# A hybrid decoder layer on one core: another order of the mixer's products

## The chip, the cores and the metric

The kernel runs on one core of one Trainium2 chip. The metric is the device time of one execution in microseconds; three executions of the kernel before gave 1690.62, 1692.16 and 1694.79 us (median 1692.16).

## What is computed

One inference step of one decoder layer in float32, for a prompt of 512 tokens and 8 samples of 4 tokens: 544 columns of width 1024. Cut to what matters here:

```
x += 0.5 * SwiGLU_1(rms(x))                  # feed-forward, width 2816
u  = rms(x) @ w_in                           # one combined projection
A: sliding-window attention, 12 heads of 128 in 3 groups (dilation 1, 4, 16),
   the three heads of a slot merged by their softmax denominators
B: gated delta rule, 8 heads of 128, causal convolution of width 4 on q/k/v,
   chunked exact form, head norm, gate silu(z)
x += (sig(gA) * (oA @ w_proj_a) + sig(gB) * (oB @ w_proj_b)) @ w_out
x += 0.5 * SwiGLU_2(rms(x));   y = rms(x)
```

The outputs are y, the new keys and values, the convolution rows and the delta-rule states, for prompt and samples.

## The kernel before

Activations stand transposed, features on the 128 partitions and the 544 columns in two halves h of 272. A *unit* is one 128-row block of one product for one half: 8 (or 4, or 11) weight tiles of 128x128, three matmuls per tile. Weights and activations are split in a rounded part and a rest (`split_next`, line 428; tiles G, xh, xl, hh), and a unit sums hi*hi, hi*lo and lo*hi, so one tile costs three matmuls of 272 columns. `unit` (line 613) issues them. The weights of four tiles form a group G: ACT rounds it, VectorE or GpSimd subtracts to get the rest.

`make_plan` (line 155) writes down the units: first feed-forward, then `ba` (the two logits of the delta rule), then the mixer, then the output projections `pa`, `pb`, `wo`, then the second feed-forward. The mixer's order is the table `MIX_ORDER` (line 43): ("a", i) stands for attention head i = 3*slot + group, that is the six units q, k, v times two halves; ("p", i) for delta-rule head i, six units; ("z", n) for the gate block n of the delta rule, two units; ("t", n) for the four units of output gate n. Unit names below are those of the plan: `gdn 4 2 0` is delta-rule head 4, its third product (v), half 0; `at 3 2 1 0` is slot 3, group 2, key, half 0; `z 0 1` and `gate 3 1 1` end with the half.

The work behind the products (*side work*) is written as generators: `conv`, `gating`, `gdn_pair` (two delta-rule heads at a time), `gdn_sample`, `attn_slot`, `attn_sample`. A generator yields between its steps. After every weight tile `unit` calls `pump` (line 647), which lets those generators go one step that a planner (class `Meter`) holds to be ready; their matmuls then stand in TensorE's queue between two matmuls of the unit. Storage of 544 columns (tag S, `CFG["S"]` tiles) is counted in `live`; a generator that needs tiles yields in `need` (line 288) until there is room. Where a unit itself cannot go on (its convolution buffers are full, or `z_load` cannot reserve its tiles) `until` (line 294) calls `force` (line 667), which lets the side work run, step behind step, until the condition holds. TensorE's queue is in order.

The norms: `norm_acc` (538) squares on ACT and adds on GpSimd, `norm_fin` (584) sums over the partitions by a matmul with ones and takes the inverse square root on VectorE (`rsqrt`, 392). At the start eight weight groups are split ahead, then the first norm runs while the first units already multiply. `store_y` (605) is the last norm's multiplication. All engine calls go through one line of `Meter` (line 122), so every row of the profile shows L122; tiles tell the rows apart.

Names in the rows: mm, sd are PSUM tiles; X, Y, Pm, Q, B are tiles of the triangular solve in `gdn_pair`, vk its values, r the inverse norm (or a remainder in `gdn_pair`); cache, ex, pT belong to `attn_sample`; st, mk, zm, kf to `gdn_sample`; astf to the merge in `attn_slot`; bas and g to `gating`; mats holds the identity (transposes) and other constants.

Of the kernel before, what the change touches and what calls it, by code (L numbers as in the profile page):

```python
# [17 lines left out]
P = 128  # L18
DM = 1024
KT = 8  # L20
# [18 lines left out]

CFG = dict(S=62, S2=4, G=4, G2=8, RAW=2, U3=3, H=10, HM=6, LA=4, LAG=3.0, SLACK=0.0, BANKS=3, PRE=3, LOV=("pa", "pb", "ba", "z", "gate", "gdn", "at"), CV=0, WARM=4, EP=8, DUE=2, RES=0, RQ="gpsimd")  # L40


MIX_ORDER = [("a", 0), ("p", 0), ("p", 1), ("p", 2), ("a", 1), ("p", 3), ("a", 2), ("a", 3), ("p", 4), ("a", 4), ("p", 5), ("a", 5)]
MIX_ORDER += [("p", 6), ("a", 6), ("p", 7), ("a", 7), ("a", 8), ("a", 9), ("a", 10), ("a", 11)]
MIX_ORDER += [("z", n) for n in range(6)] + [("t", n) for n in range(4)] + [("z", n) for n in (6, 7)]

# [159 lines left out]
def consts():  # L206
# [35 lines left out]
    m4 = ((i % 4)[:, None] == np.arange(4)[None, :]).astype(np.float32)  # L242
    mats = np.concatenate([ident, tri, negm, tri_s, neg_s, ones_s, m1, one, hb, mb, mh, cs, by4, by4.T, m4], 1)
    at = np.concatenate(t0 + [t1, t2, ts], 1)
# [18 lines left out]
class Builder:  # L263
# [214 lines left out]
    def build(self):  # L478
        nc, A = self.nc, self.A
        self.x = [self.S(name="x") for _ in range(KT)]  # L480
        vec = self.C([P, A["in_vec_dram"].shape[1]], name="vec")
        mats = self.C([P, A["in_mats_dram"].shape[1]], name="mats")
        warm = self.H()
        nc.gpsimd.memset(warm, 0.0)
# [15 lines left out]
        for _ in range(CFG["WARM"]):  # L500
            self.mm(ps[:, :NH], warm[:, 0:P], warm)
        names = ["ident", "tri", "negm", "tri_s", "neg_s", "ones_s", "m1", "ones"]
        for k, n in enumerate(names):
# [9 lines left out]
        self.gn = vec[:, 196:197]  # L513
        self.acc, self.r = [None, None], [None, None]
        self.xn = [(self.S(dt=F32R, name="xh"), self.S(dt=F32R, name="xl")) for _ in range(KT)]
# [6 lines left out]
        xw = lambda n, h: self.xw_tile(n, h, 0)  # L522
        seq(xw, 0, {3: (0,), 5: (1,), 7: (0, 1)})
        load_x(1, range(4, KT))
# [13 lines left out]
    def norm_acc(self, n, h):  # L538
        s = self.sl(h)
        if n == 0:  # L540
            self.acc[h] = [self.S([P, NH], name="acc")]
            self.act(self.acc[h][0], self.x[n][:, s], AF.Square)
        else:
            q = self.H()
            self.act(q, self.x[n][:, s], AF.Square)
            if self.last and n == KT - 1 and h == 1:
                self.acc[h].append(q)
            else:
                self.tt(self.acc[h][0], self.acc[h][0], q, ALU.add, self.nc.gpsimd)
        if self.last:  # L550
            self.act(self.x[n][:, s], self.x[n][:, s], AF.Copy, scale=self.wn[3][:, n:n + 1])
# [53 lines left out]
    def store_y(self, h):  # L605
        s = self.sl(h)
        for n in range(KT):
            f = self.H()
            self.tt(f, self.x[n][:, s], self.R(h), ALU.mult, self.nc.gpsimd if n % 3 == 2 else None)
            (self.nc.scalar if n % 2 and h else self.nc.sync).dma_start(self.A["out_y"][:, n, s], f)  # L610
# [70 lines left out]
    def kernel_units(self):  # L681
# [5 lines left out]
        self.xn2, self.normed = [], [False, False]  # L687
        self.use, self.norm_no = [False, False], 0
        for ui, u in enumerate(self.units):
# [8 lines left out]
            pend.append(getattr(self, "u_" + u[0])(*u[1:]))  # L698
            if ui in (3, 6):
                self.norm_fin(ui // 3 - 1)  # L700
            if ui not in (3, 6) and ui < 6:
                continue
# [102 lines left out]
    def u_ba(self, h, wids):  # L805
        ps = self.unit(wids, self.xn, h)

        def evac():
            self.tt(self.bas[:40, self.sl(h)], ps[:40], self.R(h)[:40], ALU.mult)
            if h == 1:  # L810
                self.spawn(self.gating(), self.bas)
        return evac

# [1049 lines left out]
```

## Time and profile before

| | before |
|---|---|
| median of 3 executions | 1692.16 us (1690.62 to 1694.79) |
| the profiled execution | 1692.98 us |
| its span, first to last instruction | 1691.2 us |
| mean granted TensorE clock | 0.985 |
| TensorE busy | 1646.0 us (97%) |
| VectorE, ACT, GpSimd busy | 1010.5, 622.4, 164.5 us |
| moved by DMA | 204.66 MB |

How to read it: PE rows are matmuls, PEld rows the weight loads that overlap them, DVE is VectorE, POOL is GpSimd. PEclk is the granted clock as a share of full speed. A time in square brackets behind a row is how long the engine stood idle just before it, and what ended that.

### The profile page before, as it was taken

The numbers are of one execution on the slowest core, as the hardware profiler recorded it, in microseconds if no ns is written. First come the engines' busy times: TensorE is split into PE (matmuls) and PEld (weight loads), VectorE is DVE, ScalarE is ACT, GpSimd is POOL, SyncE is SP. The second block draws the span as 40 slices with busy tenths as digits, with TensorE's granted clock in tenths as the row PEclk, the third lists the DMA queues.
The fourth block names the chain that finished last, engine by engine and source line by source line (L and its number), as shares of the span: only waits on it lengthen the run. The fifth ranks groups of instructions, "written<-read, shape, count | busy, mean of one in ns | idle before, by whom it ended". The sixth has DMA issues, their size and how long they took to land.

```text
span 1691.2 us, 33645 instructions
## 1 busy us (share of the span) xinstructions
PE 1646.0 (97%) x13389; PEld 1603.8 (95%) x13389; DVE 1010.5 (60%) x2497; ACT 622.4 (37%) x1559; POOL 164.5 (10%) x289
## 2 busy tenths in 40 slices
PE   7999999999999989999999999999999999999996
PEld 7999999999899978988989888999999999999996
DVE  7755255545777977578867467263357554355534
ACT  5332223333454434453534345332243332133332
POOL 5000000001012121022121110000010000000012
PEclk9999999999999979999999999999999999999998
DMA  5222222221524543367455856232332322222221
GB/s 184 84 92 88 91 85 93 83 88 63 174 88 126 191 142 123 125 192 219 132 167 180 292 185 190 88 103 88 119 120 76 100 88 88 88 90 86 93 77 59
DMA packets 105649, 204.66 MB, mean 121 GB/s; under 512 B 20434, under 2 KB 46580, under 8 KB 105492
## 3 DMA queue, kind: packets, MB, share of 16 engines
q1 hardware_dynamic: 93924, 161.97, 29.6%
q0 software_dynamic: 10992, 39.99, 7.7%
q8 instruction: 105, 1.72, 0.4%
q10 hardware_dynamic: 576, 0.56, 0.1%
q14 instruction: 52, 0.43, 0.1%
HBM read 172.04 MB, written 30.43 MB: 120 GB/s over the span
## 4 chain that ended last, share of the span: by engine, by line
PE 88%; DVE 6%; DMA 2%; ACT 2%; issue 1%; SPq 1%; DVEq 0%; POOL 0%; ACTq 0%
PE mm L122 44%; PE sd L122 43%; DVE H L122 1%; SPq L122 1%; DVE G L122 1%; DVE xl L122 1%; DMA qkv<-qd 1%; ACT s L122 0%; DVE r L122 0%; DVE y L122 0%; DVE ast L122 0%; DMA raw<-in_W_dram 0%; DMA x<-in_x_dram 0%; ACT G L122 0%; DMA st<-in_ssm_dram 0%
## 5 line engine op out<-in xcount | busy, mean ns | idle before, releaser
L122 PE MATMUL mm<-xh,G 128*128 128x272 f32 x3632 | 733.7, 293 | 5.0 <-DVE G L122 2.0
L122 PEld LDWEIGHTS mm<-xh,G 128*128 128x128 f32 x3632 | 585.0, 189 | 19.3 <-issue 10.7
L122 PE MATMUL mm<-xl,G 128*128 128x272 f32 x1816 | 524.5, 289 | 0.4 <-DVE xl L122 0.4
L122 DVE TENSOR_TENSOR G<-raw,G 128x512 fp32r<-128x512 f32 x468 | 303.4, 691 | 184.0 <-ACT G L122 178.2
L122 PE MATMUL sd<-xh,G 128*128 128x272 f32 x1904 | 363.1, 288 | 0.0
L122 PEld LDWEIGHTS mm<-xl,G 128*128 128x128 f32 x1816 | 344.0, 189 | 1.5 <-DVE xl L122 0.6
L122 ACT ACTIVATE G<-raw 128x512 fp32r<-128x512 f32 x474 | 272.0, 622 | 100.5 <-PE mm L122 46.6
L122 PEld LDWEIGHTS sd<-xh,G 128*128 128x128 f32 x1904 | 300.0, 188 | 0.2
L122 PE MATMUL sd<-xl,G 128*128 128x272 f32 x952 | 273.6, 287 | 0.0
L122 PEld LDWEIGHTS sd<-xl,G 128*128 128x128 f32 x952 | 179.1, 188 | 0.1
L122 PE MATMUL sd<-hh,G 128*128 128x272 f32 x1287 | 162.9, 288 | 0.0
L122 PEld LDWEIGHTS sd<-hh,G 128*128 128x128 f32 x1287 | 161.7, 188 | 0.1
L122 POOL TENSOR_TENSOR acc<-acc,H 128x272 f32<-128x272 f32 x55 | 44.6, 811 | 910.6 <-ACT H L122 909.4
L122 ACT ACTIVATE hh<-H 128x272 fp32r<-128x272 f32 x88 | 38.0, 431 | 201.7 <-DVE H L122 201.7
L122 PE MATMUL mm<-hh,G 128*128 128x272 f32 x825 | 104.6, 287 | 0.0
L122 PEld LDWEIGHTS mm<-hh,G 128*128 128x128 f32 x825 | 103.7, 188 | 0.0
L122 ACT ACTIVATE H<-H 128x272 f32<-128x272 f32 (+1 forms) x89 | 38.2, 429 | 162.3 <-DVE H L122 162.3
L122 POOL DMA_DIRECT2D raw<-in_W_dram x76 | 41.5, 546 | 507.1 <-DVE G L122 292.0
L122 DVE SCALAR_TENSOR_TENSOR H<-H,H 128x272 f32<-128x272 f32 x120 | 54.5, 454 | 28.2 <-ACT H L122 27.5
L122 DVE SCALAR_TENSOR_TENSOR x<-sd,x 128x272 f32<-128x272 f32 x49 | 21.4, 439 | 78.0 <-PE sd L122 78.0
L122 DVE SCALAR_TENSOR_TENSOR y<-U,vec,y 128x568 f32<-128x568 f32 x72 | 63.3, 880 | 7.6 <-ACT y L122 4.8
L122 DVE TENSOR_TENSOR hh<-H,hh 128x272 fp32r<-128x272 f32 x88 | 39.0, 443 | 43.8 <-ACT hh L122 43.8
(269 smaller groups left out, 1774.9 us busy)
## 6 DMA issues: line engine op xcount, KB each, us to landing
raw<-in_W_dram SPq DMA_DIRECT2D x161, 512.0 KB, 3.5
raw<-in_W_dram POOLq DMA_DIRECT2D x76, 512.0 KB, 4.1
qkv<-qd SPq DMA_DIRECT2D x36, 256.0 KB, 4.7
st<-in_ssm_dram SPq DMA_DIRECT2D x32, 256.0 KB, 4.9
cache<-in_kc_dram SPq DMA_DIRECT2D x28, 256.0 KB, 4.8
cache<-in_vc_dram SPq DMA_DIRECT2D x28, 256.0 KB, 3.9
qd<-av SPq DMA_DIRECT2D x24, 256.0 KB, 2.2
out_dram<-av SPq DMA_DIRECT2D x24, 256.0 KB, 3.3
```

The costliest lines, as they stand in the source:

```text
L122: r = f(*args, **kw)
```

## The change

A new order of the mixer: heads a 4 and a 0 come first, a 6 and a 7 between p 4 and p 5, the z blocks and the gates t are mixed, and a 11, which completes the last slot, comes behind z 0, z 1 and z 2. One more tile of storage S (63, with S2=3). At the start the weight rests that GpSimd subtracted go to VectorE (EP=0, and 0 in place of 1 in the table of the first splits), two more warm matmuls, the matrix of ones is set by memset, the last addition of each half of the first norm is left to TensorE's sum, and the first `norm_fin` comes after three units in place of four. The gating step starts 2.5 us later in the planner's time. At the end all eight multiplications of the second half go to VectorE.

```
-CFG = dict(S=62, S2=4, G=4, G2=8, RAW=2, U3=3, H=10, HM=6, LA=4, LAG=3.0, SLACK=0.0, BANKS=3, PRE=3, LOV=("pa", "pb", "ba", "z", "gate", "gdn", "at"), CV=0, WARM=4, EP=8, DUE=2, RES=0, RQ="gpsimd")
-MIX_ORDER = [("a", 0), ("p", 0), ("p", 1), ("p", 2), ("a", 1), ("p", 3), ("a", 2), ("a", 3), ("p", 4), ("a", 4), ("p", 5), ("a", 5)]
-MIX_ORDER += [("p", 6), ("a", 6), ("p", 7), ("a", 7), ("a", 8), ("a", 9), ("a", 10), ("a", 11)]
-MIX_ORDER += [("z", n) for n in range(6)] + [("t", n) for n in range(4)] + [("z", n) for n in (6, 7)]
+CFG = dict(S=63, S2=3, G=4, G2=8, RAW=2, U3=3, H=10, HM=6, LA=4, LAG=3.0, SLACK=0.0, BANKS=3, PRE=3, LOV=("pa", "pb", "ba", "z", "gate", "gdn", "at"), CV=0, WARM=6, EP=0, DUE=2, RES=0, RQ="gpsimd")
+MIX_ORDER = [
+    ("a", 4), ("a", 0), ("p", 0), ("p", 1), ("p", 2), ("a", 1), ("p", 3), ("a", 3), ("a", 2), ("p", 4), ("a", 6),
+    ("a", 7), ("p", 5), ("a", 5), ("p", 6), ("p", 7), ("a", 10), ("a", 9), ("a", 8), ("z", 0), ("t", 3), ("z", 1),
+    ("z", 2), ("a", 11), ("t", 2), ("z", 3), ("t", 1), ("z", 4), ("z", 5), ("z", 6), ("z", 7), ("t", 0),
+]
...
+        self.ones = self.C([P, P], name="ones")
+        nc.gpsimd.memset(self.ones, 1.0)
...
-        seq(xw, 0, {3: (0,), 5: (1,), 7: (0, 1)})
+        seq(xw, 0, {3: (0,), 5: (0,), 7: (0, 0)})
...
-            if self.last and n == KT - 1 and h == 1:
+            if self.last and n == KT - 1 and h == 1 or self.norm_no == 0 and n == KT - 1:
                 self.acc[h].append(q)
...
-            self.tt(f, self.x[n][:, s], self.R(h), ALU.mult, self.nc.gpsimd if n % 3 == 2 else None)
+            self.tt(f, self.x[n][:, s], self.R(h), ALU.mult, self.nc.gpsimd if n % 3 == 2 and h == 0 else None)
...
-            if ui in (3, 6):
-                self.norm_fin(ui // 3 - 1)
-            if ui not in (3, 6) and ui < 6:
+            if ui in (2, 6):
+                self.norm_fin(ui // 6)
+            if ui != 3 and ui < 6:
                 continue
...
                 self.spawn(self.gating(), self.bas)
+                self.side[-1][1] += 2.5
```

TensorE's queue at the first solve of a delta-rule pair. Before, at the end of unit gdn 4 2 0:

```order
L122 MATMUL mm_7283<-xh_4961,G_7162 128x272
L122 MATMUL sd_7337<-X_7316,B_6102 128x64 x4
L122 MATMUL sd_7337<-X_7320,B_6164 128x64 x4
L122 MATMUL sd_7352<-Y_6977,Pm_7317 128x64 x4
L122 MATMUL sd_7352<-Y_6983,Pm_7321 128x64 x4
L122 MATMUL sd_7365<-astf_7349,mats_80 128x32
L122 MATMUL sd_7365<-astf_7348,mats_80 128x32
L122 MATMUL sd_7374<-X_7316,B_6102 64x64 x4
L122 MATMUL sd_7374<-X_7320,B_6164 64x64 x4
L122 MATMUL sd_7393<-Y_6977,Q_7383 64x64 x4
L122 MATMUL sd_7393<-Y_6983,Q_7383 64x64 x4
L122 MATMUL sd_7420<-vk_5638,Y_6977 128x128
```

The same steps in the changed kernel, inside the same unit:

```order
L124 MATMUL sd_7439<-X_7392,B_6301 128x64 x4
L124 MATMUL sd_7439<-X_7396,B_6360 128x64 x4
L124 MATMUL sd_7458<-kq_6493 128x256 x2
L124 MATMUL sd_7300<-st_7292,mk_7298 32x128 x4
L124 MATMUL sd_7300<-st_7292,mk_7299 32x128 x4
L124 MATMUL mm_7432<-xh_4747,G_7331 128x272
L124 MATMUL mm_7432<-xl_4748,G_7331 128x272
L124 MATMUL mm_7432<-xh_4747,G_7331 128x272
L124 MATMUL sd_7478<-Y_7164,Pm_7393 128x64 x4
L124 MATMUL sd_7478<-Y_7170,Pm_7397 128x64 x4
L124 MATMUL sd_7300<-st_7294,mk_7298 32x128 x4
L124 MATMUL sd_7300<-st_7294,mk_7299 32x128 x4
```

Before, no product stands between the steps, and 62 rows follow each other before the next product; now products of the unit stand between each two steps.

TensorE's queue at the solve of the last pair. Before, at the end of unit z 0 1:

```order
L122 MATMUL mm_12101<-xh_4961,G_11957 128x272
L122 MATMUL sd_11304<-cache_11708,ex_11297 32x256 x2
L122 MATMUL sd_11304<-cache_11868,ex_11298 32x64 x8
L122 MATMUL sd_12153<-smp_4656 32x32 x12
L122 MATMUL sd_12177<-mats_80,av_11987 128x128 x4
L122 MATMUL sd_12185<-X_11989,B_10788 128x64 x4
L122 MATMUL sd_12185<-X_11993,B_10854 128x64 x4
L122 MATMUL sd_12198<-zm_12009,kf_11750 128x512
L122 MATMUL sd_12213<-Y_11694,Pm_11990 128x64 x4
L122 MATMUL sd_12213<-Y_11700,Pm_11994 128x64 x4
L122 MATMUL sd_12229<-astf_12208,mats_80 128x32
L122 MATMUL sd_12229<-astf_12207,mats_80 128x32
```

In the changed kernel the last pair is solved in units z 2 1 and at 3 2 0 0:

```order
L124 MATMUL sd_12130<-X_12079,B_11040 128x64 x4
L124 MATMUL sd_12130<-X_12083,B_11111 128x64 x4
L124 MATMUL sd_11775<-cache_11909,ex_11768 32x256 x2
L124 MATMUL mm_12106<-xh_4921,G_11894 128x272
L124 MATMUL mm_12106<-xl_4922,G_11894 128x272
L124 MATMUL mm_12106<-xh_4921,G_11894 128x272
L124 MATMUL sd_11775<-cache_11924,ex_11768 32x256 x2
L124 MATMUL mm_12106<-xh_4983,G_11894 128x272
L124 MATMUL mm_12106<-xl_4984,G_11894 128x272
L124 MATMUL mm_12106<-xh_4983,G_11894 128x272
L124 MATMUL sd_12161<-Y_11850,Pm_12080 128x64 x4
L124 MATMUL sd_12161<-Y_11856,Pm_12084 128x64 x4
```

Six products stand where before there was one side matmul.

VectorE's queue at the first norm, its root and the first unit's evacuation. Before (the four subtractions G stand in GpSimd's queue instead):

```order
L122 TENSOR_TENSOR H_360<-r_361 128x272
L122 SCALAR_TENSOR_TENSOR H_360<-H_360,H_359 128x272
L122 SCALAR_TENSOR_TENSOR r_361<-H_360,r_361 128x272
L122 TENSOR_TENSOR H_371<-mm_241,r_361 128x272
L122 SCALAR_TENSOR_TENSOR H_372<-H_372,H_371 128x272
```

Now:

```order
L124 SCALAR_TENSOR_TENSOR H_322<-H_322,H_321 128x272
L124 SCALAR_TENSOR_TENSOR r_323<-H_322,r_323 128x272
L124 TENSOR_TENSOR G_333<-raw_158,G_333 128x512
L124 TENSOR_TENSOR G_336<-raw_158,G_336 128x512
L124 TENSOR_TENSOR G_341<-raw_179,G_341 128x512
L124 TENSOR_TENSOR G_344<-raw_179,G_344 128x512
L124 TENSOR_TENSOR H_374<-mm_243,r_323 128x272
```

The four subtractions moved from GpSimd to VectorE, behind the root and ahead of the evacuation.

## Rows read from the trace of the kernel before

**Rows 1.** The page's first part: busy us, share of the span, instructions.
```profile
PE 1646.0 (97%) x13389; PEld 1603.8 (95%) x13389; DVE 1010.5 (60%) x2497; ACT 622.4 (37%) x1559; POOL 164.5 (10%) x289
```

**Rows 2.** Table of stretches: stretch, length, busy us by engine, PEclk, DMA share, GB/s.
```profile
0.00:40.00 40.00, 31.25 (x193) 28.87 (x194) 29.37 (x42) 21.39 (x49) 22.22 (x26) 0.92 0.59 194
40.00:400.00 360.00, 360.00 (x2877) 360.00 (x2877) 190.69 (x381) 111.74 (x231) 7.77 (x10) 1.00 0.28 87
400.00:455.00 55.00, 50.51 (x393) 48.91 (x392) 39.34 (x111) 18.68 (x49) 5.05 (x9) 1.00 0.36 118
455.00:605.00 150.00, 149.60 (x1178) 148.19 (x1177) 123.43 (x349) 71.49 (x215) 23.52 (x55) 1.00 0.45 141
605.00:645.00 40.00, 33.66 (x268) 29.48 (x267) 27.79 (x90) 13.86 (x44) 6.99 (x17) 0.74 0.33 106
645.00:750.00 105.00, 103.92 (x963) 98.05 (x962) 69.02 (x226) 50.65 (x162) 17.49 (x35) 1.00 0.47 146
750.00:795.00 45.00, 39.02 (x260) 33.26 (x259) 40.02 (x105) 19.25 (x52) 11.55 (x21) 0.92 0.78 242
795.00:960.00 165.00, 164.26 (x1475) 154.93 (x1474) 117.16 (x374) 67.64 (x204) 28.06 (x56) 1.00 0.56 180
960.00:985.00 25.00, 21.28 (x210) 19.13 (x208) 17.07 (x62) 10.60 (x34) 4.07 (x5) 0.86 0.63 215
985.00:1060.00 75.00, 74.11 (x673) 65.96 (x671) 48.39 (x147) 39.93 (x114) 8.69 (x16) 1.00 0.65 203
```

**Rows 3.** TensorE in order of time (start us, us, row, idle before), near 610.
```profile
609.20 2.51 PE L122 MATMUL sd<-X,B 128*128 128x64 f32 x16 [2.42 <-DVE X L122]
```

**Rows 4.** Waits of TensorE, 605 to 985: us in total, times, longest.
```profile
PE sd L122 <- DVE Pm L122: 3.4, 2, 2.8
...
PE sd L122 <- ACT vk L122: 2.9, 1, 2.9
```

**Rows 5.** TensorE in order of time, the first 40 us.
```profile
2.29 4.00 PE L122 MATMUL sd<-H 128*128 128x272 f32 x8 [2.29 <-ACT H L122]
8.16 0.39 PE L122 MATMUL mm<-xh,G 128*128 128x272 f32 x1 [1.88 <-ACT G L122]
...
35.16 0.70 PE L122 MATMUL mm<-acc,mats 128*128 128x272 f32 x2 [3.22 <-DVE H L122]
37.01 0.59 PE L122 MATMUL mm<-xh,G 128*128 128x272 f32 x1 [1.16 <-DVE H L122]
```

**Rows 6.** The chain that ended last, in order of time: start us, us, what.
```profile
37.01 4.79 PE mm L122 x24
...
56.84 9.00 PE mm L122 x72
```

**Rows 7.** VectorE, then GpSimd, in order of time, the first 40 us.
```profile
11.51 0.69 DVE L122 TENSOR_TENSOR G<-raw,G 128x512 fp32r<-128x512 f32 x1
...
27.86 1.34 DVE L122 TENSOR_TENSOR H<-r 128x272 f32<-128x272 f32 x1
...
33.55 0.44 DVE L122 SCALAR_TENSOR_TENSOR H<-H,H 128x272 f32<-128x272 f32 x1
...
27.55 5.67 POOL L122 TENSOR_TENSOR G<-raw,G 128x512 fp32r<-128x512 f32 x4
```

**Rows 8.** VectorE in order of time, the end of the kernel.
```profile
1683.19 3.35 DVE L122 TENSOR_TENSOR H<-x,r 128x272 f32<-128x272 f32 x6
```

**Rows 9.** The page's DMA issues: count, KB each, us from issue to landing.
```profile
st<-in_ssm_dram SPq DMA_DIRECT2D x32, 256.0 KB, 4.9
cache<-in_kc_dram SPq DMA_DIRECT2D x28, 256.0 KB, 4.8
```

**Rows 10.** TensorE in order of time, at the mixer's entry.
```profile
427.70 0.32 PE L122 MATMUL sd<-mats,bas 40*128 40x40 f32 x2 [2.24 <-DVE bas L122]
```

More of the change, by code (lines that the diff above doesn't have):

```diff
@@ L242, in consts @@
     m4 = ((i % 4)[:, None] == np.arange(4)[None, :]).astype(np.float32)
-    mats = np.concatenate([ident, tri, negm, tri_s, neg_s, ones_s, m1, one, hb, mb, mh, cs, by4, by4.T, m4], 1)
+    mats = np.concatenate([ident, tri, negm, tri_s, neg_s, ones_s, m1, hb, mb, mh, cs, by4, by4.T, m4], 1)
     at = np.concatenate(t0 + [t1, t2, ts], 1)
@@ L501, in build @@
             self.mm(ps[:, :NH], warm[:, 0:P], warm)
-        names = ["ident", "tri", "negm", "tri_s", "neg_s", "ones_s", "m1", "ones"]
+        names = ["ident", "tri", "negm", "tri_s", "neg_s", "ones_s", "m1"]
         for k, n in enumerate(names):
@@ L513, in build @@
         self.gn = vec[:, 196:197]
-        self.acc, self.r = [None, None], [None, None]
+        self.acc, self.r, self.norm_no = [None, None], [None, None], 0
         self.xn = [(self.S(dt=F32R, name="xh"), self.S(dt=F32R, name="xl")) for _ in range(KT)]
@@ L687, in kernel_units @@
         self.xn2, self.normed = [], [False, False]
-        self.use, self.norm_no = [False, False], 0
+        self.use = [False, False]
         for ui, u in enumerate(self.units):
```

## The prediction

> **What bounds the kernel now.** Read the page's first part, then one table of stretches, then the waits inside the stretches that lose time. TensorE is busy 1646.0 us, 97% of the span, and VectorE 60% [rows 1]; the reader is to see that only TensorE's own holes and its slow spells can give time back. The table of stretches [rows 2] says where they are. From 40 to 400 us (the first feed-forward block) TensorE has no idle time and the granted clock is 1.00: nothing to gain. The losses stand in the first 40 us (8.75 us idle), at the entry of the mixer (400 to 455: 4.49 idle), and in three short stretches inside the mixer: 605 to 645 (33.66 busy of 40), 750 to 795 (39.02 of 45) and 960 to 985 (21.28 of 25), together 6.34 + 5.98 + 3.72 = 16.04 us. The four long stretches between them lose 0.40, 1.08, 0.74 and 0.89 us.
>
> In the same three stretches the granted clock reads 0.74, 0.92 and 0.86, and 1.00 in the rest of the mixer. With two levels (1.2 and 2.4 GHz) a reading g means that 2(1-g) of the stretch ran at the lower one, where work takes twice as long, so (1-g) of the busy time was lost: 0.26 x 33.66 + 0.08 x 39.02 + 0.14 x 21.28 = 8.75 + 3.12 + 2.98 = 14.85 us. Idle and clock together cost **30.9 us** there, the largest part of what TensorE loses anywhere.
>
> Why there? In the longest of them TensorE stands in a chain of small products: a delta-rule pair waits 2.42 us for VectorE's transposed tile X [rows 3]. In the waits over the whole piece the longest single ones are Pm (2.8 us) and ACT's vk (2.9 us) [rows 4], again steps of that chain and of the head norms at its end. These are latencies: they cost nothing when mixer products stand between two steps, and cost all of it when none do. The first order fence shows the cause: before, 62 rows of side work stand at the end of the unit gdn 4 2 0 without one product between; the second largest run is the 23 rows behind z 0 1, the third 16 rows behind gdn 7 2 0. Those are the three stretches.
>
> **The change, part by part.**
>
> *The order of the units, with one more S tile.* The products, the side steps and their sizes are the same; only what stands between two steps moves. In the changed order the 62-row run is gone: between X<-B and Y<-Pm of the same pair stand three products and six side rows, and the later steps have products between them too. The 23 rows behind z 0 1 are gone as well (second fence: 6 products between the same two steps of the last pair). The longest runs left are 15, 10 and 9 rows, and the 15 hold two independent groups (eight products of one attention block, then transposes), not a chain. One short chain is left without products, 7 rows at the end of gate 3 1 1 (two cache products, two solver steps, the transposes of vk). I price it by the nearest row, the stretch 960 to 985: 3.72 idle + 2.98 clock = 6.7 us. The rest of the lengthened side work I price at nothing, because the four long stretches, 495 us with such work spread among products, lose 3.1 us in all. If that cover fails, the price per uncovered pair is a stretch like 750 to 795 (5.98 + 3.12 = 9.1 us). Gain: 30.9 - 6.7 = **24.2 us**; ends 0 (all the holes reappear) and 30.9.
>
> What is late next: the side work now runs to the last gate unit, 57 products ahead of the first output projection. At 0.125 us each (9.00 us for 72, [rows 6]) that is 7.1 us of cover for the last copies, so nothing is charged there. The entry: the transposes of bas, which waited 2.24 us for VectorE [rows 10], now come 18 products (2.25 us) later, so that wait goes. But the gating chain behind it is a VectorE chain of the same length, and the products that need it come sooner (the g rows stand 123 products behind the bas transposes, 159 before). What is saved is waited for again: 0, with ends of -2.2 and +2.
>
> *The start.* TensorE's hole from 32 to 37 us: the second norm sum waits 3.22 us and the next unit 1.16 us for VectorE [rows 5]. VectorE is in the inverse square root, and four of its operations take from 27.86 to 33.55 us, 1.4 us each, while GpSimd subtracts four weight groups (5.67 us from 27.55); the next operation of the same size, with GpSimd idle, takes 0.44 [rows 7]. The change (EP=0) puts these four subtractions on VectorE, behind the root (third fence). The root's four operations then fall from 5.7 to 4 x 0.44 = 1.8 us, saving 3.9; the integer step before them (not shown) should save a little too. The four subtractions cost 4 x 0.69 = 2.8 us [rows 7]. That is -1.1, and about -1 more for the shorter GpSimd work ahead (at the first norm the last addition of each half goes to TensorE): **-2 us**; ends +1 (a root that stays half slow) and -4 (the slow spell behind the hole goes too: 24 products take 4.79 us at 37.01 where 72 take 9.00 later [rows 6], 1.8 us).
>
> Here a rule speaks against the edit: the Trainium skill, Perfetto Trace Analysis, section Optimizing Scalar/DVE Operations, says that work may be offloaded from a saturated VectorE to GpSimd. By that rule the move the other way adds 4 x 0.69 = 2.8 us to the chain that TensorE waits for, and the total would come out near 1671 us. The same section adds that the two engines share a read port, so that the offload might not help; the rows of 1.4 against 0.44 us look like this second case. Either way the time lies inside the forecast's own range below.
>
> *Two more warm products.* Eight passes take 4.00 us from 2.29; four more end at 8.3, and the first real product starts at 8.16 behind its weights [rows 5]: 0 to +0.3. The extra norm products (four instead of two, at the very first norm) fall into the hole that is left. *The end:* eight output multiplications on VectorE at 0.44 instead of six in 3.35 us beside GpSimd [rows 8]: +0.2. *ones by memset, EP, S2:* no TensorE work; nothing waits on them after the first microseconds.
>
> **Sum.** 1692.98 (the profiled execution) - 24.2 - 2.0 + 0.2 = 1667.0. The median of the runs shown is 0.8 us below that execution, so the forecast is **1666 us**.
>
> How much is there to win is also a matter of the measure. The holes above are those of the product rows: 16.04 us idle in the three stretches. The Trainium skill, Perfetto Trace Analysis, section Identifying the Most-Contended Engine, holds the products' busy share for a poor measure and judges by the weight loads. By those the three stretches are idle 10.5 + 11.7 + 5.9 = 28.1 us, 12.1 more, and the sum would be 1654. The stretch 795 to 960 decides against it here: weight loads are idle 10 us of 165 there while the products are idle 0.74 [rows 2], so idle loads are no waiting. Its time goes in with the first rival below.
>
> **Rivals.**
> - *Everything goes.* The chain at gate 3 1 1 is covered and the clock stays up at the start: 1692.2 - 30.9 - 4 = **1657**. For it: in the long stretches clock and products hold. Against: seven rows of chain remain.
> - *Only the long run pays.* The 62 rows are spread (6.34 + 8.75 = 15.1 us), but VectorE, 40.02 us busy of 45 in 750 to 795 [rows 2], is late there for its own load and not for the order, and the end keeps its wait: 1692.2 - 15.1 - 2 = **1675**. For it: VectorE's 89% in that stretch. Against: it also follows runs of 8 and 16 rows.
> - *It does not do what it says.* Heads are held back by S tiles; with one more of 63 the stop may only move to another unit, and the holes come back where the order puts no products: **1690**. Against: the order's rows themselves, no run over 15.
> - *Slower.* TensorE takes its queue in order, and the cache and st products now stand between mixer products: a load that lands late then stops the products too. 60 such steps (32 st, 28 keys, landing 4.9 and 4.8 us after issue [rows 9]) at 0.6 us each are 36 us: 1692.2 - 26 + 36 = **1702**. It decides from 0.45 us a step, where the gain is eaten. Against: in the waits from 605 to 985 none of TensorE's is put down to a load; the longest are those of [rows 4].
>
> **Chances.** The forecast (1660 to 1674) 0.55; everything goes 0.13; only the long run (1674 to 1684) 0.20; no change 0.05; slower 0.07. A measurement of this kernel can tell about 0.3%, 5 us. So faster 0.88, same 0.05, slower 0.07. The range reaches from the full gain with a saved entry wait, 1655, to 1684, where only the long run pays and half of the start is lost; that leaves out about 0.15.
>
> **What the new profile would show.** Right: no stretch of 40 us in the mixer with TensorE under 36 busy, granted clock 1.00 but for one or two dips, side products until some 7 us before the first output projection, VectorE's operations of the first norm at 0.44 us and the start's hole near 3 us. Wrong: a new stretch like 605 to 645, or waits of cache and st products on DMA that add up to over 10 us. The largest doubt is the 6.7 us left for new uncovered chains.

## The result and the profile after

The changed kernel takes **1664.78 us** (median of 4 executions, 1664.0 to 1667.46) against 1692.06 of the kernel before in the same session; the ratio is 0.984, with a 95% interval of 0.9823 to 0.9857. The profiled execution is 1664.81 us, its span 1663.0. The forecast was 1666.

The page's first part, to be read beside [rows 1]:

```profile
PE 1633.3 (98%) x13397; PEld 1595.3 (96%) x13397; DVE 1005.7 (60%) x2505; ACT 621.7 (37%) x1559; POOL 153.1 (9%) x280
```

The table of stretches of the changed kernel (columns as in [rows 2]):

```profile
0.00:40.00 40.00, 34.71 (x234) 31.91 (x235) 28.80 (x54) 21.70 (x50) 12.30 (x19) 1.00 0.57 193
40.00:400.00 360.00, 359.88 (x2879) 359.66 (x2879) 191.65 (x380) 113.78 (x234) 8.53 (x11) 1.00 0.28 88
400.00:460.00 60.00, 54.46 (x411) 53.04 (x410) 39.65 (x109) 19.04 (x49) 4.47 (x7) 0.94 0.41 136
460.00:600.00 140.00, 139.99 (x1111) 139.31 (x1110) 102.78 (x291) 66.93 (x202) 19.86 (x49) 1.00 0.40 121
600.00:700.00 100.00, 99.35 (x940) 92.13 (x940) 70.21 (x234) 40.43 (x112) 21.54 (x46) 1.00 0.56 176
700.00:800.00 100.00, 98.66 (x841) 92.41 (x840) 85.68 (x241) 54.38 (x174) 20.77 (x39) 1.00 0.61 196
...
900.00:930.00 30.00, 26.32 (x218) 24.95 (x217) 23.46 (x85) 15.59 (x45) 4.68 (x11) 0.91 0.50 148
```

The reader is to see three things. The three mixer stretches of [rows 2] with 33.66 of 40, 39.02 of 45 and 21.28 of 25 are gone: from 460 to 800 TensorE is idle 2.00 us in 340. One short hole is left, 900 to 930, with 3.68 us idle at a granted clock of 0.91. And the entry, 400 to 460, has 5.54 us idle at 0.94, where [rows 2] has 4.49 idle at 1.00: this place became worse.

The waits of TensorE from 600 to 1070 us in the changed kernel (in total, times, longest), beside [rows 4]:

```profile
PE sd L124 <- DVE srz L124: 3.7, 2, 2.5
PE sd L124 <- DVE Y L124: 1.3, 1, 1.3
PE sd L124 <- DVE as L124: 1.2, 1, 1.2
PE sd L124 <- DVE X L124: 0.6, 1, 0.6
```

Pm and vk, the longest of before, are no longer in the list; these four lines are the whole of it. Names that the rows below need: srz and sBA are tiles of the solve in `gdn_sample`, as of the softmax in `attn_sample`, av of a new attention head, beta and LA of `gating`; oh is the rounded part of a gated delta-rule output, which an output projection reads.

To see where time went, I take the start of the same weight product in both traces (the rows with G as weights; there are 11376 in each kernel, and their number per stage is the same). The difference of those starts, after minus before, is worked out at number 3168 (the first of the `ba` units), 3405 (mixer under way), 7000 (output projections) and 11375 (the last), and the spans give the end.

| stage | time in the kernel before | predicted | measured |
|---|---|---|---|
| start, up to product 3168 | 0 to 414.25 | -2.0 | -4.27 |
| entry, to 3405 | to 452.54 | 0 | +2.91 |
| mixer, to 7000 | to 1127.04 | -24.2 | -25.79 |
| second feed-forward, to 11375 | to 1676.94 | 0 | -0.22 |
| end | to 1691.16 | +0.2 | -0.75 |

Together -28.1 us, the difference of the spans (1691.16 and 1663.04 us). The size came out, and two errors, start and entry, nearly cancelled; that part was luck.

### The profile page after: what moved, and what is told of

Its sections match the earlier page's. It is cut to its first block, busy times and chain, and to the rows that moved or that the text cites. A ratio compares the mean times of both kernels' runs of the same rounds, so it can differ in the third digit from the quotient of the medians.

```text
span 1663.0 us, 33659 instructions
## 1 busy us (share of the span) xinstructions
PE 1633.3 (98%) x13397; PEld 1595.3 (96%) x13397; DVE 1005.7 (60%) x2505; ACT 621.7 (37%) x1559; POOL 153.1 (9%) x280
## 4 chain that ended last, share of the span: by engine, by line
PE 90%; DVE 6%; DMA 1%; ACT 1%; issue 1%; SPq 1%; DVEq 0%; ACTq 0%
PE mm L124 46%; PE sd L124 44%; DVE H L124 1%; DVE G L124 1%; SPq L124 1%; DVE r L124 1%; DVE Yc L124 1%; DVE inv L124 1%; DVE nrm L124 0%; DMA raw<-in_W_dram 0%; DVE xl L124 0%; ACT H L124 0%; DMA basd<-bas 0%; DVE y L124 0%; ACT xh L124 0%
## 5 line engine op out<-in xcount | busy, mean ns | idle before, releaser
L124 PE MATMUL mm<-xh,G 128*128 128x272 f32 x3632 | 745.2, 294 | 4.2 <-DVE g L124 2.5
```

The costliest lines, as they stand in the source:

```text
L124: r = f(*args, **kw)
```

## The experiments

All stages below are differences to the kernel before, as in the table above, in us; the ratio is to the kernel before on the same chip.

| kernel | median us | ratio [95%] | start | entry | mixer |
|---|---|---|---|---|---|
| changed kernel | 1664.78 | 0.9840 [0.9823, 0.9857] | -4.27 | +2.91 | -25.79 |
| order alone | 1700.1 | 1.0042 [1.0027, 1.0057] | +0.06 | +0.80 | +8.00 |
| storage alone | 1672.27 | 0.9881 [0.9864, 0.9897] | +0.12 | -0.36 | -20.07 |
| order and storage | 1666.32 | 0.9844 [0.9829, 0.9859] | +0.33 | +0.55 | -26.64 |
| changed, old order | 1677.35 | 0.9909 [0.9894, 0.9924] | -4.87 | +1.42 | -12.54 |
| three edits undone | 1663.58 | 0.9828 [0.9813, 0.9842] | -4.07 | +0.44 | -26.71 |
| rests on GpSimd | 1666.6 | 0.9841 [0.9826, 0.9856] | -2.58 | +3.72 | -27.29 |
| later LA | 1662.44 | 0.9817 [0.9802, 0.9831] | -4.45 | -0.14 | -25.15 |
| a stop put back | 1693.32 | 1.0004 [0.9995, 1.0013] | -4.54 | +3.36 | +1.46 |
| a 11 early | 1659.32 | 0.9794 [0.9779, 0.9808] | -4.29 | +2.72 | -31.43 |
| a 6, a 7 late | 1700.7 | 1.0039 [1.0025, 1.0053] | -3.85 | +3.75 | +7.99 |
| a 4 late | 1678.42 | 0.9907 [0.9892, 0.9922] | -4.49 | +3.95 | -13.82 |
| later LA, t 3 first | 1660.26 | 0.9800 [0.9786, 0.9815] | -4.69 | -0.15 | -24.46 |

### Order and storage, apart and together

The new order in the kernel before, nothing else:

```
-MIX_ORDER = [("a", 0), ("p", 0), ("p", 1), ("p", 2), ("a", 1), ("p", 3), ("a", 2), ("a", 3), ("p", 4), ("a", 4), ("p", 5), ("a", 5)]
...
+MIX_ORDER = [
+    ("a", 4), ("a", 0), ("p", 0), ("p", 1), ("p", 2), ("a", 1), ("p", 3), ("a", 3), ("a", 2), ("p", 4), ("a", 6),
...
```

> The kernel before with the new order table alone (62 S tiles, all other edits undone). In TensorE's queue the longest runs of side rows without a product are 21 and 14 rows of chain (solver steps and their tails) and 13 and 11; before they were 62, 23 and 16. Theory (a chain of small products costs its latencies and the slow clock behind them when no product stands between its steps, and nothing when products do): two chains of the size of the stretch 960 to 985 stay, 6.7 us each, so 1692 - 30.9 + 13.4 = 1675 us, with the holes at those two runs. Rival (the additional S tile is what lets the heads go on, the order by itself does little): 1690 us. Rival (the edits at the start and the end carry the gain): 1692 us.

One more S tile in the kernel before, nothing else (in `CFG`):

```
-S=62, S2=4
+S=63, S2=3
```

> The kernel before with one more S tile alone (S=63, S2=3), old order. The run of 62 side rows behind gdn 4 2 0 stays, the longest others fall from 23 and 16 to 11 rows. Theory: the 62 rows keep their 6.34 + 8.75 = 15.1 us, the other two stretches (5.98 + 3.12 and 3.72 + 2.98 us) go in good part: 1677 to 1685 us. Rival (storage pays by itself): 1668 us. Rival (storage matters only with the order): 1690 us.

Both of these diffs together, without the edits at the start, the entry and the end:

> The kernel before with the new order and one more S tile, without the edits at the start and the end and without the later gating. The side rows stand among the products as in the changed kernel (longest runs 15, 10, 9). Theory: the whole mixer gain of about 26 us, without the 4.3 us of the start and the 0.8 us of the end: 1669 to 1671 us. Rival (the edits at the start pay more than their own 4.3 us, since they set when the weight groups and GpSimd come free): 1675 us or more.

The changed kernel with `MIX_ORDER` of before, that is, the first diff of this section the other way round:

> The changed kernel with the old order table, all other edits kept. Its longest runs of side rows are 46 (in the last z units) and 12. Theory: the run of 46 rows costs between 6.7 us (the short chain's price) and 15.1 us (the price of the 62 rows before): 1672 to 1680 us. Rival (the order is what pays and storage nothing): 1692 - 4.3 - 0.8 = 1687 us. Rival (the order adds nothing to the rest): 1665 us.

Measured: 1700.1, 1672.27, 1666.32 and 1677.35 us; only the last lies in the range of its theory. My theory was that the order removes the holes and the tile helps. That fell: **the tile alone gives 20.07 of the 25.79 us, the order alone costs 8.00**, and the order is worth 6.57 more (26.64 - 20.07) only once the tile is there. Beside the changed kernel's other edits it is worth 13.25 (25.79 - 12.54): with the old order those edits cost 7.5 us of the mixer (20.07 - 12.54). That they do it by shifting the planner's times, and with them the stops, is argued and not tried apart. By the medians order and storage together are not told apart from the changed kernel (the intervals of the ratios overlap): that the edits at the start, the entry and the end shorten the whole is not shown. With 62 tiles the holes did not go, they moved from 605 to 645 (where the kernel before has them) to 885 to 970. Stretches of the kernel with the order alone:

```profile
600.00:700.00 100.00, 99.38 (x941) 92.17 (x940) 71.58 (x240) 40.75 (x113) 22.61 (x46) 1.00 0.56 179
...
900.00:930.00 30.00, 18.02 (x96) 16.00 (x95) 17.23 (x51) 3.21 (x8) 6.11 (x8) 0.60 0.43 121
930.00:970.00 40.00, 32.70 (x229) 30.92 (x228) 31.07 (x100) 13.76 (x43) 9.31 (x16) 0.87 0.45 130
```

TensorE of the same kernel in order of time (columns as in [rows 3]) inside that hole:

```profile
899.66 0.66 PE L124 MATMUL sd<-mats,av 128*128 128x128 f32 x4 [0.46 <-ACT av L124]
903.88 0.33 PE L124 MATMUL sd<-mats,srz 128*128 128x128 f32 x1 [3.56 <-ACT srz L124]
911.01 3.76 PE L124 MATMUL sd<-X,B 128*128 128x64 f32 x16 [6.81 <-DVE X L124]
915.36 3.67 PE L124 MATMUL sd<-Y,Pm 128*128 128x64 f32 x16 [0.59 <-DVE Pm L124]
919.88 1.97 PE L124 MATMUL sd<-X,B 128*64 128x64 f32 x16 [0.85 <-DVE X L124]
```

It is the pair's solve with no product between its steps, as in [rows 3]: 6.81 us of waiting for X, and X,B takes 3.76 us for 16 matmuls, where the changed kernel, with products between, takes 1.89 without a wait (TensorE in order of time, last pair):

```profile
942.12 1.89 PE L124 MATMUL sd<-X,B 128*128 128x64 f32 x16
...
946.11 1.89 PE L124 MATMUL sd<-Y,Pm 128*128 128x64 f32 x16
```

So the mechanism held and my measure of it did not: I took the length of a run of side rows for its price. The kernel with the storage alone keeps the 62-row run, yet its stretch is cheaper than before, 5.86 us idle and 0.07 x 94.14 = 6.6 us of clock:

```profile
600.00:700.00 100.00, 94.14 (x857) 87.87 (x856) 73.21 (x222) 42.08 (x121) 20.44 (x44) 0.93 0.48 144
```

and the run of 14 rows in the order-alone kernel, 899.66 to 926.27, costs far more than the 6.7 us that I had put down for it: 12.4 us idle in its six waits, before the clock is counted. The tile adds no memory: it is one of the four of S2, which the feed-forward blocks and the output projections use and the mixer does not. What it does follows from the program: `z_load` waits in `reserve` until tiles are free, and while it waits only side steps are issued. Counted as the program writes its queues, 172 and 89 side steps are issued in the stops at z 0 0 and z 1 0 with the new order and 62 tiles, 17 (at z 1 0 alone) with 63.

### Does a stop put back cost what it should?

```
             pend.append(getattr(self, "u_" + u[0])(*u[1:]))
+            if u[:4] == ("gdn", 4, 2, 0):
+                self.until(lambda: 0 in self.heads)
```

> The changed kernel with one statement more: at unit gdn 4 2 0 the side work must run until the first pair of heads is done, so that a run of 67 side rows stands in TensorE's queue without a product, with the new order, the storage and the start as they are. Theory (a chain without products costs its idle time and the clock behind it): a hole like that of before at 605 to 645, 12 to 16 us, the end later by as much, 1677 to 1681 us. Rival (TensorE has so much side work later that what is done early is saved later): within 3 us of the changed kernel, 1665 to 1668 us.

Measured 1693.32 us: the mixer is 27.25 us longer than in the changed kernel, all of the gain, and twice what I expected. The stretch of this kernel that holds the stop:

```profile
600.00:700.00 100.00, 80.52 (x756) 70.16 (x755) 71.88 (x239) 32.55 (x91) 20.34 (x42) 0.90 0.52 163
```

TensorE in order of time at the longest wait there:

```profile
666.40 1.30 PE L124 MATMUL sd<-mats,as 128*128 128x128 f32 x5 [8.14 <-DVE as L124]
```

Idle 19.48 plus clock 0.10 x 80.52 = 8.05 make 27.5 us in this stretch. The same sum over all stretches from 460 to 1110 us gives 40.7 in this kernel and 10.0 in the changed one, 30.7 apart where 27.25 were measured: the way of pricing (idle plus the busy time lost to the clock) is good to an eighth here, and better in short stretches (26.6 apart in slices of 10 us). So one stop put into the changed order costs all that the change gains. It is not the hole of before, though. The first pair's solve is over before the hole begins, with 15 products inside (TensorE, its last step):

```profile
629.87 0.29 PE L124 MATMUL mm<-xh,G 128*128 128x272 f32 x1
629.99 0.60 PE L124 MATMUL sd<-vk,Y 128*128 128x128 f32 x4
630.35 0.37 PE L124 MATMUL mm<-xh,G 128*128 128x272 f32 x1
```

What the stop uncovers are the steps behind the solve, `gdn_sample` and the sample attention's softmax (as, 8.14 us), which I had not counted.

### Each move undone

First a 11 directly behind a 8:

```
-    ("a", 7), ("p", 5), ("a", 5), ("p", 6), ("p", 7), ("a", 10), ("a", 9), ("a", 8), ("z", 0), ("t", 3), ("z", 1),
-    ("z", 2), ("a", 11), ("t", 2), ("z", 3), ("t", 1), ("z", 4), ("z", 5), ("z", 6), ("z", 7), ("t", 0),
+    ("a", 7), ("p", 5), ("a", 5), ("p", 6), ("p", 7), ("a", 10), ("a", 9), ("a", 8), ("a", 11), ("z", 0), ("t", 3), ("z", 1),
+    ("z", 2), ("t", 2), ("z", 3), ("t", 1), ("z", 4), ("z", 5), ("z", 6), ("z", 7), ("t", 0),
```

> The changed kernel with one move undone: a 11 follows a 8 directly, ahead of z 0, in place of standing behind z 2. No run of side rows in TensorE's queue is longer than 15 (15, 11, 10), as in the changed kernel. But the program stops at the z products more often: counted as it writes the queues, 148 side steps are issued while unit z 0 0 waits for its tiles, where the changed kernel has 17 at z 1 0; the new order with 62 tiles has 172 at z 0 0 and 89 at z 1 0 and lost some 35 us there. Theory A (the runs of rows without a product tell the price): 1665 to 1668 us. Theory B (the stop tells it, at 0.05 to 0.13 us a step, since its steps wait for each other through VectorE whatever their rows): 131 steps more, 1671 to 1682 us, with the holes at z 0 0, near 880 to 930 us.

Then a 6 behind p 6 and a 7 behind p 7:

```
-    ("a", 4), ("a", 0), ("p", 0), ("p", 1), ("p", 2), ("a", 1), ("p", 3), ("a", 3), ("a", 2), ("p", 4), ("a", 6),
-    ("a", 7), ("p", 5), ("a", 5), ("p", 6), ("p", 7), ("a", 10), ("a", 9), ("a", 8), ("z", 0), ("t", 3), ("z", 1),
+    ("a", 4), ("a", 0), ("p", 0), ("p", 1), ("p", 2), ("a", 1), ("p", 3), ("a", 3), ("a", 2), ("p", 4),
+    ("p", 5), ("a", 5), ("p", 6), ("a", 6), ("p", 7), ("a", 7), ("a", 10), ("a", 9), ("a", 8), ("z", 0), ("t", 3), ("z", 1),
```

> The changed kernel with another move undone: a 6 behind p 6 and a 7 behind p 7, as before, in place of between p 4 and p 5. Longest runs of side rows 27, 19, 13 and 11; 126 side steps are issued in stops at gdn 5 1 0 and 5 2 0 and 189 at z 0 0 and z 1 0. Theory A (runs of rows): the 27 and the 19 rows cost 7 us each, 1675 to 1681 us. Theory B (stops): 300 steps more than the changed kernel at 0.05 to 0.13 us, 1680 to 1704 us, the larger part at z 0 0 and z 1 0. Rival (the place of a 6 and a 7 does not matter): 1665 us.

And a 4 behind p 4:

```
-    ("a", 4), ("a", 0), ("p", 0), ("p", 1), ("p", 2), ("a", 1), ("p", 3), ("a", 3), ("a", 2), ("p", 4), ("a", 6),
+    ("a", 0), ("p", 0), ("p", 1), ("p", 2), ("a", 1), ("p", 3), ("a", 3), ("a", 2), ("p", 4), ("a", 4), ("a", 6),
```

> The changed kernel with the third move undone: a 0 comes first and a 4 behind p 4. Longest runs of side rows 12, 9 and 9; stops with 62 side steps at z 1 0, 33 at z 3 0, 27 at p 7. Theory A (runs of rows): 1665 to 1668 us. Theory B (stops): 100 steps more at 0.05 to 0.13 us, 1670 to 1678 us. Rival (the delta rule's heads come one head earlier, which is what sets the rest): 1660 us.

Measured 1659.32, 1700.7 and 1678.42 us. Both counts fail as a price. The kernel with a 11 early has the same longest run of 15 rows and 131 more steps in its stops, and is **faster** than the changed kernel (the intervals of the ratios don't overlap); the one with a 4 late has no run over 12 rows and is slower, by 13.6 us. For a 6 and a 7 late and a 4 late the totals lie near or in the range of the stops (theory B: 1680 to 1704 and 1670 to 1678), which, with a 11 early against it, is no support for a price by the step.

Part of what separates the kernels is seen in the traces of all 14 (56 solves of a pair). I take a solve from its first X,B row to its first vk,Y row and count what stands between; the idle time includes the wait just before the X,B row, the length and the time at the lower clock do not:

| solves | products between | length us | idle us | at the lower clock, us |
|---|---|---|---|---|
| 5: before (first, last pair), order alone, storage alone, a 6 and a 7 late | 0 | 12.3 to 15.6 | 3.72 to 8.42 | 6.8 to 14.4 |
| 51, all others | 12 to 93 | 11.4 to 20.7 | 0 to 1.66 | 0 |

Every solve without a product costs, and none of the others has more than 1.66 us of idle time. That explains a part of the order alone and of a 6 and a 7 late: idle time and half of the busy time at the lower clock make 14.8 us in the one solve and 11.3 in the other, where the mixers are 34.6 us longer than with order and storage and 33.8 longer than in the changed kernel. In the latter's solve at 907 us (TensorE, in order of time) the X,B row reads like the one above:

```profile
907.30 3.68 PE L124 MATMUL sd<-X,B 128*128 128x64 f32 x16 [2.95 <-DVE X L124]
```

It explains neither a 4 late nor the stop put back, whose four solves each are covered. With a 4 late TensorE's largest wait comes ahead of a solve, between cache rows:

```profile
936.34 0.47 PE L124 MATMUL sd<-mats,srz 128*128 128x128 f32 x1 [7.45 <-ACT srz L124]
```

A wider count takes these in: every stretch of more than 6 us from one weight product to the next, whatever stands in it. From 460 to 1110 us such stretches hold 12.97 of 19.15 us of idle time in the kernel before, 18.5 of 26.1 with the order alone, 25.2 of 29.6 with the stop put back and 11.3 of 17.6 with a 4 late; outside them 3.0 to 7.6 us are left in every one of the 14 kernels. Length is still no price: one stretch of 8.8 us in the changed kernel with the old order, at 599 us, has no idle time at all.

With a 11 early, the hole that the changed kernel kept is nearly gone. TensorE of the changed kernel in that hole:

```profile
923.75 0.49 PE L124 MATMUL sd<-srz,sBA 128*128 128x128 f32 x2 [2.54 <-DVE srz L124]
...
925.94 0.80 PE L124 MATMUL sd<-srz,sBA 128*128 128x128 f32 x2 [1.14 <-DVE srz L124]
```

The same stretch with a 11 early, to be read beside the last line of the changed kernel's table:

```profile
900.00:930.00 30.00, 28.94 (x239) 27.60 (x238) 23.27 (x92) 15.09 (x47) 5.80 (x14) 1.00 0.61 191
```

And TensorE there, in order of time:

```profile
921.34 0.39 PE L124 MATMUL sd<-srz,sBA 128*128 128x128 f32 x2
921.56 0.82 PE L124 MATMUL sd<-qkv,qkv 128*128 128x128 f32 x4
922.98 0.49 PE L124 MATMUL sd<-srz,sBA 128*128 128x128 f32 x2 [0.59 <-DVE srz L124]
```

The attention slot's qkv rows, there earlier because a 11 is, stand between the chain's steps. So the move of a 11 behind z 0, z 1 and z 2, one of the moves that the change consists of, cost the changed kernel 5.64 us of its mixer (31.43 - 25.79). Rows of other generators are no sure cover, though: the last solve of the kernel before has 31 of them inside and still lost 3.72 us.

The one more move on top of the later LA was meant to take the same hole away:

```
-    ("a", 7), ("p", 5), ("a", 5), ("p", 6), ("p", 7), ("a", 10), ("a", 9), ("a", 8), ("z", 0), ("t", 3), ("z", 1),
+    ("a", 7), ("p", 5), ("a", 5), ("p", 6), ("p", 7), ("a", 10), ("a", 9), ("a", 8), ("t", 3), ("z", 0), ("z", 1),
```

> The kernel with the later LA (1662.4 us) with one more move: the four units of output gate 3 come ahead of z 0, not between z 0 and z 1. The stop at z 1 0 falls from 17 side steps to 3; one of 14 steps appears at z 3 0. Theory (the hole at the end of gate 3 1 1, 3.3 us idle and 6.8 us at the lower clock, comes from the 17 steps): it goes in part or whole, 1656 to 1660 us. Rival (the last pair's solve is late by its own length, and the stop moves on to the later z units): 1662 to 1666 us.

1660.26 us, 0.9800 [0.9786, 0.9815] beside 0.9817 [0.9802, 0.9831] without the move: not told apart. By stages the mixer is 0.69 us longer, not shorter. The hole at gate 3 1 1 is gone, but its time was lost again, in part at other waits; TensorE of this kernel, in order of time:

```profile
968.82 0.77 PE L124 MATMUL sd<-mats,as 128*128 128x128 f32 x5 [1.89 <-DVE as L124]
...
1077.26 0.39 PE L124 MATMUL sd<-oh,G 128*128 128x272 f32 x1 [1.00 <-ACT oh L124]
```

The wait for as was 1.2 us without the move, and the second row is an output projection, which now waits for the last copies. Neither expectation is met: 1660.26 lies between the two ranges, the hole went as the theory said, and the rival's stop at the later z units is not seen as a stretch without products (none is longer than 4 us).

### The start and the entry

Three edits undone at three places: the gating's delay, two of the warm matmuls (in `CFG`), GpSimd's multiplications at the end:

```
-WARM=6
+WARM=4
...
-            self.tt(f, self.x[n][:, s], self.R(h), ALU.mult, self.nc.gpsimd if n % 3 == 2 and h == 0 else None)
+            self.tt(f, self.x[n][:, s], self.R(h), ALU.mult, self.nc.gpsimd if n % 3 == 2 else None)
...
-                self.side[-1][1] += 2.5
```

> The changed kernel with three edits undone that act at three separate places: the gating step is not held back by 2.5 us (mixer's entry), four warm matmuls instead of six (start), GpSimd takes its two multiplications of the second half again (end). The mixer's order of rows stays. Theory (the later gating makes the two waits of 2.5 us at the entry and the spell at the lower clock behind them): from the first ba unit to 460 us about 0.5 us are lost in place of 2.9; the start stays within 0.3 us, the end costs 0.8 us more: 1663 us. Rival (the new order makes the entry's waits, because the products that need g come sooner): entry unchanged, 1665 to 1666 us.

The planner is told that LA is ready 4.0 us later:

```
         self.spawn(self.spill())
+        self.nc.ready[LA.tensor.name] = (self.nc.ready[LA.tensor.name][0] + 4.0, "sync")
         yield LA
```

> The changed kernel with one number of the planner changed in the gating: the tile LA, which comes back through a DMA, is taken to be ready 4.0 us later, so that VectorE's steps that need it are queued later and less stands behind them. Theory (the wait of 2.5 us at 443 us comes from VectorE standing in its queue before LA's data, with the copies that TensorE needs behind it): the entry loses 0 to 1 us in place of 2.9, 1661 to 1663 us. Rival (the gating chain's own length is what TensorE waits for): the waits stay or grow, 1665 to 1669 us.

The weight rests of the start go back to GpSimd (the first line in `CFG`):

```
-EP=0
+EP=8
...
-        seq(xw, 0, {3: (0,), 5: (0,), 7: (0, 0)})
+        seq(xw, 0, {3: (0,), 5: (1,), 7: (0, 1)})
```

> The changed kernel with the subtractions of the first weight groups given back to GpSimd (EP=8, the table of the first splits as before); the other edits at the start stay. Theory (VectorE's root is slow because GpSimd works beside it): the root's four operations take about 1.4 us each again, the second norm sum or the unit behind it waits 2 to 4 us longer, and the end is later by as much, 1667 to 1669 us. Rival 1 (the norm's last addition and the earlier norm are what saved the 4.3 us): 1665 us, start unchanged. Rival 2 (what the start wins is waited for again at the mixer's entry, as the run with order and storage alone suggests, which had no gain at the start and only 0.5 us of loss at the entry): start 3 us later, entry 2 us shorter, 1665 to 1666 us.

TensorE at the entry of the changed kernel, in order of time:

```profile
438.81 0.37 PE L124 MATMUL mm<-xh,G 128*128 128x272 f32 x1 [2.52 <-DVE g L124]
...
443.36 1.11 PE L124 MATMUL sd<-mats,av 128*128 128x128 f32 x4 [2.48 <-DVE av L124]
```

VectorE just ahead of the first of them:

```profile
434.57 0.18 DVE L124 TENSOR_SCALAR beta<-beta 128x34 f32<-128x34 f32 x1 [1.89 <-ACT beta L124]
```

VectorE stands 1.89 us before beta, with the tiles for the next products queued behind it; the gating chain then runs into two waits of TensorE. Without the 2.5 us of delay the entry costs +0.44 in place of +2.91, although the wait for bas of [rows 10] is back (TensorE, three edits undone):

```profile
423.64 0.32 PE L124 MATMUL sd<-mats,bas 40*128 40x40 f32 x2 [2.24 <-DVE bas L124]
```

With LA queued later, it costs -0.14, and one wait is left (TensorE of that kernel):

```profile
440.59 0.75 PE L124 MATMUL sd<-mats,av 128*128 128x128 f32 x4 [3.28 <-DVE av L124]
```

and VectorE's beta row has no idle time before it any more. Both entries are as the theory said, to 0.14 us. By the medians neither kernel is told apart from the changed one (the intervals overlap); the stages carry the finding. That the stand before beta is what makes the two waits is argued, not shown: VectorE of the kernel before stands there nearly as long,

```profile
438.76 0.18 DVE L122 TENSOR_SCALAR beta<-beta 128x34 f32<-128x34 f32 x1 [1.64 <-ACT beta L122]
```

and TensorE's longest wait within 15 us behind it is 0.74 us.

The start: with the rests on GpSimd it is 1.69 us later, less than the 2 to 4 I expected, and 0.81 us more are lost at the entry, so the rival that the entry gives it back fell too. But the mixer is 1.50 us and the end 0.87 us shorter in this kernel's trace, the span is the same to 0.1 us and the ratios are 0.9841 and 0.9840: what the start wins is not seen in the total. One of VectorE's four slow operations of the root in that kernel:

```profile
27.21 1.41 DVE L124 SCALAR_TENSOR_TENSOR H<-H,H 128x272 f32<-128x272 f32 x1
```

GpSimd beside it:

```profile
26.84 5.84 POOL L124 TENSOR_TENSOR G<-raw,G 128x512 fp32r<-128x512 f32 x4
```

VectorE in the changed kernel, with the four subtractions behind the root:

```profile
28.98 0.44 DVE L124 SCALAR_TENSOR_TENSOR r<-H,r 128x272 f32<-128x272 f32 x1
29.34 2.49 DVE L124 TENSOR_TENSOR G<-raw,G 128x512 fp32r<-128x512 f32 x4
```

## Why the prediction was right, and where it was not

- **Mixer, -24.2 against -25.79.** The three stretches that the sum priced at 30.9 us are gone, and one short hole stayed where the prediction put it, at the end of gate 3 1 1: 3.68 us idle, and 0.09 x 26.32 = 2.4 us of clock up to 930, a little more behind it, against the 6.7 taken from [rows 2]. The number came out; what failed is the heading of that step, "the order of the units, with one more S tile", priced as one thing: the tile carries 20 us by itself, and the order without it loses 8. Of the three runs of side rows that the step names as the cause, the one of 62 stays with the tile alone, and yet most of the gain is there. The rival "it does not do what it says" described this very thing (the stop moves to another unit), and with 62 tiles it is what happened. The argument against it, "no run over 15", was no argument: the kernel with a 4 late has none over 12.
- **Start, -2 against -4.27.** Mis-sized. The subtractions were priced at -1.1 and gave 1.69. The other 2.6 us are left for the edits of the first norm and for the slow spell behind the hole, which went (not tried apart): the granted clock of the first 40 us is 1.00, not 0.92 [rows 2], and it is 1.00 with the rests on GpSimd too, so the spell did not go by the subtractions. I had that as the end of the range and took the smaller value. The hole that was to stay near 3 us is one wait of 0.41. The extra norm products were not free on the way, as their sum waits 1.49 us for GpSimd, but this fell into the hole, and TensorE goes on at 34.19 where it went on at 37.01 [rows 5] (TensorE of the changed kernel):

```profile
19.72 0.72 PE L124 MATMUL sd<-acc,ones 128*128 128x272 f32 x2 [1.49 <-POOL acc L124]
...
34.19 0.40 PE L124 MATMUL mm<-xh,G 128*128 128x272 f32 x1 [0.41 <-DVE H L124]
```

- **Entry, 0 against +2.91.** The step "what is saved is waited for again: 0" failed, outside its own ends. The line that delays the gating by 2.5 us was in the diff; the step counted the wait for bas that it takes away, but put no price on what the delay does to VectorE's queue and to the two waits behind it. Without it the loss is 0.44.
- **End, +0.2 against -0.75.** The sign was wrong. The eight multiplications take 2.90 us where six took 3.35 [rows 8]: each lasts 0.43 to 0.44, but one starts every 0.35 (VectorE, the end of the changed kernel):

```profile
1655.81 2.90 DVE L124 TENSOR_TENSOR H<-x,r 128x272 f32<-128x272 f32 x8
```

Their end comes 9.14 to 9.15 us behind the last product's start in all nine traces with this edit and 9.59 to 9.60 in the five without it: 0.45 us of gain. The rest is not decided, since the time from there to the end of the span varies by more (from the last product's start 12.59 to 13.48 us with the edit, 13.43 to 14.22 without).
- **Two more warm products, 0 to +0.3.** The first product starts at 8.30, 0.14 later [rows 5]; with four of them it starts at 8.16 to 8.71 in five traces, so no cost is seen.
- **The rules weighed.** The Trainium skill, Perfetto Trace Analysis, section Optimizing Scalar/DVE Operations, would offload from VectorE to GpSimd, and by that the total was to be 1671. The run that offloads again has a start 1.69 us later and no shorter total, so by this trace the offload does not pay; the Trainium skill's remark in that section, that the two engines share a read port, fits the 1.41 against 0.44 us. The measure of the Trainium skill, Perfetto Trace Analysis, section Identifying the Most-Contended Engine, by weight loads, gave 1654; the products' idle time, by 1666, was nearer to 1664.78.
- **The rivals.** "Slower", by loads in TensorE's queue, did not happen: from 600 to 1070 no wait of the changed kernel is put down to a DMA (with a 4 late one is, of 1.71 us). "Only the long run pays" and "everything goes" each lie 7 us or more away.

Not tried: 62 tiles with all the other edits, and a 11 early together with the later LA. The best kernel run is a 11 early, 1659.32 us.

## What to carry to other kernels

In these traces a chain of small matmuls costs little while products stand between its steps (at most 1.66 us of idle time in 51 solves), and its waits plus the clock behind them when a stop removes the products; look for what makes the program stop (here one storage tile) before reordering. Price a stop by which dependent chains fall into it, of every generator and not of the delta rule's solve alone, and not by how many rows or steps it holds. And give every line of a diff a price, even one that only changes a number in a planner.

## What the runs showed that was not expected

One more tile, the 63rd, is worth 20 us by itself, and an order that gains 6.6 us with it loses 8.0 without it. In all five solves without a product the granted clock stood at the lower level, 1.2 GHz, for 6.8 to 14.4 us of them, and 16 matmuls X,B took up to 3.76 us in place of 1.89; in the 51 others it stayed at 2.4 GHz. And one number in the planner, when a tile of 34 columns (LA) is taken to be ready, changed the entry by 3.05 us: VectorE no longer stands 1.89 us before a step of 0.18 us (beta), and of TensorE's two waits of 2.5 us one of 3.28 is left.
